# An attention output product made by token halves, one group to a unit

## The chip, the core and the metric

The program runs on one core of a Trainium2 chip. The core has five engines that work from queues of their own: TensorE (PE, matmuls; PEld is its weight load), VectorE (DVE), ScalarE (ACT), GpSimd (POOL) and SyncE (SP), which here only issues DMAs. Each queue runs in the order in which it was filled; engines wait for each other by semaphores. The metric is the device time of one execution in microseconds, the median of several runs. Before the change it is 1578.19 us (three runs, 1576.92 to 1581.11).

## What is computed

One layer of a diffusion transformer over 1024 latent tokens of width 1024 with 256 context tokens. What matters here is the token mixer: two attentions side by side, each of 8 query heads and 2 key heads of width 64, whose outputs are each multiplied by a weight, gated, added and multiplied by a third weight:

```python
o_a = _windowed_attention(q_a, k_a, v_a, k_a_c, v_a_c, sink)      # +-128 tokens and the context
o_b = _global_attention(q_b, k_b + context, v_b + context)        # all tokens and the context
g_a, g_b = jnp.split(jax.nn.sigmoid(gate_logits), 2, axis=-1)
return (g_a * (o_a @ w_branch_a) + g_b * (o_b @ w_branch_b)) @ w_out
```

Then come a residual with layer norm, a convolutional feed-forward block (1024 to 2 x 2816 to 1024) and a second residual with layer norm. All is float32; the kernel keeps that precision by splitting each operand into a high and a low part and using three matmuls for one (`mm3`, lines 89 to 91: high x high, high x low, low x high).

## The kernel before

The work runs in stages: the modulation and the input projections; the attention part; the merge of both attentions with `w_out`; the first layer norm; the feed-forward products; the last layer norm. The change is in the attention part.

The attention part is a list of 32 units (class `Unit`). A unit is one attention branch, one tile of 128 query tokens and one key head with its four query heads. Units 0 to 15 are the windowed branch (tile 0 key head 0, tile 0 key head 1, tile 1 key head 0, and so on), units 16 to 31 the global branch in the same order. For a unit the kernel makes scores on PE (`lat`, line 427, and for the global branch the context scores in `cxp`, line 463), scales them and finds maxima on DVE (line 458; 470 and 471 for the context), takes exponentials on ACT (line 425), and joins the two softmax parts (`norm`, line 478, with line 482 on DVE and line 486 on POOL). Then the probabilities of each 128 keys are transposed on PE (line 530) into a PSUM buffer of the tag `pt`, of which there are three, and split: ACT copies the high part (line 539), DVE subtracts it for the low part (line 540); two of the ten tiles of a global unit are instead copied by ACT (line 536) and split on POOL (lines 83 and 86). PE multiplies both with the values (lines 551 and 552). The result is put together and split on ACT, POOL and DVE (`out_step`, line 554), multiplied by the reciprocals of the row sums, which go through DRAM to be spread over partitions (`rows`, line 495, with DMAs on SP at lines 503 and 505), and stored in the tiles `O`. There are 12 buffers for `O`, while both branches together need 16 tiles, so that the tiles of the second half of the global branch reuse those of the first half of the windowed branch.

A loop over u (line 832) writes, for each u, the score steps of unit u, the preparation of the query of unit u + 2 (`qprep`, whose two halves are swapped by two DMAs on SP, lines 407 and 408), the value steps of the unit before, and filling steps, mixed by their fractions of the unit. DMAs that add blocks of the down-projection weights in DRAM (`wd_sums`) are issued at certain units.

The filling steps are the product of the windowed branch with its weight `w_branch_a`, from `branch_steps` (line 791). The weight comes in four blocks. `ld` loads one block (512 KB, tag `wraw`, one buffer) on SP and splits it on POOL into a high tile by a conversion (line 83) and a low tile by a subtraction (line 86), tag `whl` with two buffers, which is one block. `grp` makes one group: for one of eight output tiles of 128 channels and one half of 512 tokens it loads the stored gate (line 807, on SP), does four times three matmuls of 128x512 into a `pt` buffer and multiplies the result by the gate on DVE (line 814). With both halves in one list a block's steps are `ld` and four groups, twenty steps in all: sixteen groups and four loads. They are put in at u = 18 and spread over units 18 to 25, by steps (3, 3, 3, 3, 2, 2, 2, 2). At u = 31 the first block of the second branch's weight is loaded in the same buffers; its groups are made after the loop (line 867).

The order written here is not quite the order in which an engine runs. When the program is built, a planner goes through the written order with costs that it assumes for each instruction, and puts into each engine's queue what is ready, what was written earlier first. So a DMA or a split can stand far ahead of the unit in which it is written: the first weight block is loaded at 318.8 us and split at 349.7 us, well before unit 18. Only for the stages behind the attention part is PE's order the written one. On the chip, each queue then runs strictly in that order.

Of the kernel before, what the change touches and what calls it, by code (L numbers as in the profile page):

```python
# [30 lines left out]
VL = 1  # L31
NXT = 17
LAG = 3, 3
FILL_END = 26
XPOS = 2
SPAN = 0.8, 0.85
LN1_F = 3500.0, 5100.0, 100.0
# [29 lines left out]
def layer_kernel(  # L67
# [6 lines left out]
    nc = tc.nc  # L74
# [4 lines left out]
    def split(src, hi, lo, hi_eng, lo_eng):  # L79
        if hi_eng is nc.scalar:  # L80
            cast[:] = [nc.scalar.copy(hi, src).ins]  # L81
        elif hi_eng is nc.gpsimd:
            nc.gpsimd.tensor_scalar(out=hi, in0=src, scalar1=1.0, scalar2=0.0, op0=ALU.mult, op1=ALU.add)  # L83
        else:
            hi_eng.tensor_copy(hi, src)
        low[:] = [lo_eng.tensor_tensor(out=lo, in0=src, in1=hi.bitcast(F32), op=ALU.subtract).ins]  # L86

    def mm3(ps, a, b, start, stop, resumed=False):
        nc.tensor.matmul(ps, a[0], b[0], start=start, stop=False, skip_group_check=resumed)  # L89
        nc.tensor.matmul(ps, a[0], b[1], start=False, stop=False, skip_group_check=resumed)  # L90
        nc.tensor.matmul(ps, a[1], b[0], start=False, stop=stop, skip_group_check=resumed)  # L91
# [40 lines left out]
    def ht(name, shape=(P, T), dt=F32):  # L132
        hslot[name] = pool, tag = hfree.pop(0)
        return pool.tile(list(shape), dt, tag=tag, name=name, bufs=1)
# [623 lines left out]
    att = tc.alloc_tile_pool(name="att", bufs=1, side="right", reuse_waits="tile")  # L758
# [32 lines left out]
    def branch_steps(br, wsrc, halves, wpool, engs, f2s=range(4)):  # L791
        steps = []
        w = {}

        def ld(f2, key):
            r = wpool.tile([P, 8, P], F32, tag="wraw", name=f"rwb{br}_{key}", bufs=1)
            nc.sync.dma_start(r, wsrc[f2])
            h = wpool.tile([P, 8, P], R32, tag="whl", name=f"hwb{br}_{key}", bufs=2)
            l = wpool.tile([P, 8, P], R32, tag="whl", name=f"lwb{br}_{key}", bufs=2)
            split(r, h, l, *engs)  # L800
            w[f2] = h, l

        def grp(f, hf, mk):
            if (br, f) not in bT:
                bT[br, f] = ht(f"bT{br}_{f}")
            b = bT[br, f][:, hf * HALF:(hf + 1) * HALF]
            nc.sync.dma_start(b, sgd[br * KT + f][:, hf * HALF:(hf + 1) * HALF])
            wh, wl = w[f // 2]
            ps = mk(f"b{br}_{f}_{hf}")
            for j in range(4):  # L810
                k = (f % 2) * 4 + j
                a = O[br, hf, 0, j // 2][:, j % 2], O[br, hf, 1, j // 2][:, j % 2]
                mm3(ps, (wh[:, k], wl[:, k]), a, j == 0, j == 3)
            nc.vector.tensor_tensor(out=b, in0=ps, in1=b, op=ALU.mult)

        for f2 in f2s:
            steps.append(lambda f2=f2: ld(f2, f"{f2}_{halves[0]}"))
            for f in (2 * f2, 2 * f2 + 1):
                for hf in halves:
                    steps.append(lambda f=f, hf=hf: grp(f, hf, pt_tile))  # L820
        return steps

    def done(br, i, g):
        if g and i % 2:
            hput(f"Q{br}_{i - 1}")
        if g and i == NT - 1:
            hput(f"KL{br * 2}", f"KL{br * 2 + 1}")

    fill = []
    nu = len(units)  # L830
    vq = []
    for u in range(nu + 1):
        vs = []
        while vq and (vq[0] <= u - VL or vq[0] >= 16 or u >= 17):
            vs += units[vq.pop(0)].value_steps()
        ss = []
        if u < nu:
            ss = units[u].score_steps()
            if u + 2 < nu:
                ss.append(units[u + 2].qprep)  # L840
        if u == 31:
            first = branch_steps(1, w_b, (0, 1), att, (nc.gpsimd, nc.gpsimd), (0,))
            first[0]()
        if u == 18:
            fill += branch_steps(0, w_a, (0, 1), att, (nc.gpsimd, nc.gpsimd))
        nf = 0
        if u >= 18:
            nf = -(-len(fill) // (FILL_END - u)) if u < FILL_END else len(fill)
        fs = [fill.pop(0) for _ in range(nf)]
        if u < nu:  # L850
            ss = [units[u].context] + ss
        seq = []
        for lst, of, sp in ((ss, 0.0, SPAN[u >= 17]), (vs, VOFF, VSPAN), (fs, 0.0, 1.0)):
            for n, st_ in enumerate(lst):
                seq.append((of + sp * (n + 0.5) / len(lst), st_))
        for _, st_ in sorted(seq, key=lambda e: e[0]):
            st_()
        if u in DNS:
            wd_sums(*DNS[u])
        if u < nu:  # L860
            vq.append(u)
            done(units[u].br, units[u].i, units[u].g)
# [458 lines left out]
    for k in range(4):  # L1321
        steps = build(k)
        n = 2 if k < 2 else 0
# [278 lines left out]
    u, ot = [], []  # L1602
# [147 lines left out]
```

## Time and profile before

| what | value |
|---|---|
| median of the runs | 1578.19 us (1576.92 to 1581.11) |
| the profiled execution, its time | 1580.51 us |
| the profiled execution, its span | 1578.6 us |
| mean granted TensorE clock | 0.994 |
| start of the first windowed unit's output, `avs` | 364.6 us |
| global units 16 to 30, by the starts of their context reductions (line 470, DVE) up to that of unit 31 | 473.8 to 748.2 us |
| last unit's output, `avs` | 775.2 us |

The span runs from the first to the last instruction of the profiled execution. Views of the profile name an instruction by its line in the kernel, its engine, its operation and its tiles (`ptr<-ident,p` writes the tile `ptr` and reads the others; buffer numbers are left out). Where a line belongs to a helper, such as lines 81, 83 and 86 (the split) or 89 to 91 (the three matmuls), the tile tells which use it is: `hwb` and `lwb` are the high and low parts of a weight block of the branch products, `b` is the PSUM tile of a group, `bT` the gated result. A line of the waits says which instruction's engine sat idle until which other instruction ended, with the total, how often, and the longest. Busy time of PE comes from modelled ends, so that back-to-back matmuls overlap in it; the time from one start to the next is the better measure of what a matmul needs.

### The profile page before, as it was taken

How to read it: one execution, taken by the hardware profiler on the slowest of the kernel's cores; microseconds unless marked ns; L12 is line 12 of the kernel's file. 1: busy time of each engine (PE TensorE's matmuls, PEld its weight loads, DVE VectorE, ACT ScalarE, POOL GpSimd, SP SyncE). 2: the span in 40 equal slices, each digit the busy share in tenths (PEclk: the TensorE clock that was granted, in tenths of full speed). 3: DMA queues.
4: the chain of work that ended last, by engine and by line, in shares of the span. 5: the costliest groups of instructions: out<-in, count | busy, mean ns of one | idle time of the engine just before them, and what ended most of it. 6: DMA issues, size and time to landing. Idle time of an engine off the chain costs nothing.

```text
span 1578.6 us, 21930 instructions
## 1 busy us (share of the span) xinstructions
PE 1528.4 (97%) x7614; PEld 1264.6 (80%) x7614; DVE 1198.0 (76%) x1761; ACT 808.9 (51%) x1439; POOL 756.5 (48%) x737
## 2 busy tenths in 40 slices
PE   6999999999999999999999999999999999999997
PEld 5878788878886887777788898888888888888886
DVE  7797645628888777788675679888888888656797
ACT  5422222448888667688522466444444444435533
POOL 0573312426666566655432544666667765021053
PEclk9999999999999999999999999999999999999999
DMA  9685662322227555532344132333334446996723
GB/s 378 218 313 187 213 219 87 120 79 74 64 82 180 138 128 127 128 84 41 130 160 93 54 107 81 121 107 107 107 107 107 107 111 178 364 270 221 244 92 107
DMA packets 112015, 230.25 MB, mean 146 GB/s; under 512 B 13504, under 2 KB 27328, under 8 KB 111808
## 3 DMA queue, kind: packets, MB, share of 16 engines
q1 hardware_dynamic: 96464, 199.20, 37.9%
q0 software_dynamic: 10400, 20.19, 8.2%
q10 hardware_dynamic: 5040, 9.46, 1.6%
q8 instruction: 60, 0.98, 0.3%
q14 instruction: 51, 0.42, 0.1%
HBM read 177.61 MB, written 65.87 MB: 154 GB/s over the span
## 4 chain that ended last, share of the span: by engine, by line
PE 73%; DVE 12%; DMA 5%; ACT 4%; issue 3%; POOL 1%; SPq 0%; ACTq 0%; DVEq 0%; POOLq 0%
PE ptr L530 5%; PE b L91 3%; PE b L90 3%; PE b L89 3%; PE g L89 3%; PE g L91 3%; PE g L90 3%; PE s L413 2%; PE av L551 2%; PE c L90 2%; PE d L90 2%; PE a L90 2%; PE c L89 2%; PE d L89 2%; PE a L89 2%
## 5 line engine op out<-in xcount | busy, mean ns | idle before, releaser
L540 DVE TENSOR_TENSOR ptl<-ptr,pth 128x512 fp32r<-128x512 f32 x188 | 124.6, 684 | 27.8 <-ACT pth L539 25.6
L86 DVE TENSOR_TENSOR ld<-rd,hd 128x1024 fp32r<-128x1024 f32 x77 | 97.6, 1284 | 50.8 <-ACT hd L81 48.7
L530 PE MATMUL ptr<-ident,p 128*128 128x128 f32 x816 | 126.7, 278 | 9.2 <-DVE ptl L540 6.8
L539 ACT CAST pth<-ptr 128x512 fp32r<-128x512 f32 x188 | 106.5, 588 | 56.5 <-PE ptr L530 32.8
L425 ACT ACTIVATE p<-p,nm 128x1024 f32<-128x1024 f32 (+2 forms) x128 | 125.3, 981 | 11.1 <-DVE p L458 10.3
L530 PEld LDWEIGHTS ptr<-ident,p 128*128 128x128 f32 x816 | 93.6, 140 | 39.6 <-DVE ptl L540 13.9
L81 ACT CAST hd<-rd 128x1024 fp32r<-128x1024 f32 x77 | 79.4, 1050 | 88.5 <-PE p L91 60.4
L551 PE MATMUL av<-pth,VT 128*128 128x512 f32 x236 | 104.6, 443 | 1.0 <-ACT avs L557 0.5
L90 PE MATMUL p<-ld,hd 128*128 128x512 f32 x264 | 103.5, 392 | 0.3 <-DVE ld L86 0.3
L89 PE MATMUL p<-hd 128*128 128x512 f32 x264 | 103.8, 393 | 0.0
L91 PE MATMUL p<-hd,ld 128*128 128x512 f32 x264 | 103.5, 392 | 0.0
L89 PE MATMUL g<-hh,whg 128*128 128x512 f32 x256 | 99.9, 390 | 0.0
L91 PE MATMUL g<-hh,wlg 128*128 128x512 f32 x256 | 99.7, 389 | 0.0
L90 PE MATMUL g<-hl,whg 128*128 128x512 f32 x256 | 99.6, 389 | 0.0
L552 PE MATMUL av<-ptl,VT 128*128 128x512 f32 x236 | 97.7, 414 | 1.9 <-POOL ptl L86 1.8
L86 POOL TENSOR_TENSOR wlg<-wg,whg 128x512 fp32r<-128x512 f32 x32 | 44.2, 1388 | 112.7 <-ACT whg L81 109.2
L458 DVE TENSOR_SCALAR_CACHE_REDUCE p<-s,cvt,nmc 128x1024 f32<-128x1024 f32 x64 | 84.4, 1339 | 12.3 <-PE s L414 11.8
L413 PE MATMUL s<-KL,q 128*128 128x512 f32 (+2 forms) x192 | 76.0, 396 | 2.9 <-ACT p_x L425 2.0
L187 DVE CUSTOM_DVE_ANT_0 wml<-wml,sc,bmc 128x1024 f32<-128x1024 f32 x32 | 45.6, 1435 | 40.6 <-DMA wml<-in_wmodT_dram 39.7
L83 POOL TENSOR_SCALAR pth<-prw 128x512 fp32r<-128x512 f32 x48 | 31.0, 646 | 87.8 <-ACT prw L536 62.3
L414 PE MATMUL s<-KL,q 128*128 128x512 f32 (+2 forms) x192 | 71.7, 373 | 0.0
L81 ACT CAST wS<-s 128x512 fp32r<-128x512 f32 x76 | 45.3, 621 | 51.0 <-POOL s L1083 50.2
(402 smaller groups left out, 4945.7 us busy)
## 6 DMA issues: line engine op xcount, KB each, us to landing
wml<-in_wmodT_dram SPq DMA_DIRECT2D x48, 512.0 KB
ru<-in_w_up_dram SPq DMA_DIRECT2D x38, 512.0 KB
rd<-td SPq DMA_DIRECT2D x55, 256.0 KB
rd<-sd SPq DMA_DIRECT2D x44, 256.0 KB
rd<-in_w_dn_dram SPq DMA_DIRECT2D x33, 256.0 KB
wm<-in_wmodT_dram SPq DMA_DIRECT2D x16, 512.0 KB
wg<-in_w_g_dram SPq DMA_DIRECT2D x32, 256.0 KB
sgd<-sg ACTq DMA_DIRECT2D x32, 256.0 KB
```

What stands on the lines that cost most here:

```text
L81: cast[:] = [nc.scalar.copy(hi, src).ins]
L86: low[:] = [lo_eng.tensor_tensor(out=lo, in0=src, in1=hi.bitcast(F32), op=ALU.subtract).ins]
L89: nc.tensor.matmul(ps, a[0], b[0], start=start, stop=False, skip_group_check=resumed)
L90: nc.tensor.matmul(ps, a[0], b[1], start=False, stop=False, skip_group_check=resumed)
L91: nc.tensor.matmul(ps, a[1], b[0], start=False, stop=stop, skip_group_check=resumed)
L413: nc.tensor.matmul(o, self.q[0][:, hs], ks, start=True, stop=False)
L425: nc.scalar.activation(p, s, AF.Exp, bias=nm[:, h:h + 1], scale=scale, accum_out=sm[:, h:h + 1])
L530: nc.tensor.transpose(tr[:, h * P:(h + 1) * P], self.pslice(h, n), ident)
L539: nc.scalar.copy(hi, tr)
L540: nc.vector.tensor_tensor(out=lo, in0=tr, in1=hi.bitcast(F32), op=ALU.subtract)
L551: nc.tensor.matmul(self.av, v, hi, start=first, stop=False)
L552: nc.tensor.matmul(self.av, v, lo, start=False, stop=self.left == 0)
```

## The change

The product of the windowed branch is written as two lists, one for each half of the tokens, each with all four weight blocks: eight loads with their splits instead of four, and the same sixteen groups. A list has eight groups; the load of the next block is put behind each second group. The sixteen groups go into units 16 to 30, one each, and two into unit 27; the first half's groups are thus in units 16 to 23 and the second half's in units 24 to 30. The first block of the first half is loaded at unit 15, the first block of the second half with the last group of the first half, in unit 23.

```diff
@@ -31,7 +31,7 @@
 LAG = 3, 3
-FILL_END = 26
+FILL_G = {u: 1 + (u == 27) for u in range(16, 31)}
 XPOS = 2
@@ -841,12 +841,13 @@
         if u == 31:
             first = branch_steps(1, w_b, (0, 1), att, (nc.gpsimd, nc.gpsimd), (0,))
             first[0]()
-        if u == 18:
-            fill += branch_steps(0, w_a, (0, 1), att, (nc.gpsimd, nc.gpsimd))
-        nf = 0
-        if u >= 18:
-            nf = -(-len(fill) // (FILL_END - u)) if u < FILL_END else len(fill)
-        fs = [fill.pop(0) for _ in range(nf)]
+        fs = [st_ for _ in range(FILL_G.get(u, 0)) for st_ in fill.pop(0)]
+        if u == 15:
+            for hf in (0, 1):
+                st_ = branch_steps(0, w_a, (hf,), att, (nc.gpsimd, nc.gpsimd))
+                lds, grps = st_[0::3], [g for n, g in enumerate(st_) if n % 3]
+                fill += [[g] + lds[n // 2 + 1:n // 2 + 2] * (n % 2) for n, g in enumerate(grps)]
+                (fs if hf == 0 else fill[7]).append(lds[0])
         if u < nu:
             ss = [units[u].context] + ss
```

## The prediction, made before the changed kernel was run

> **What bounds the kernel now.** I read the page first, for the whole. Its first, engine and chain lines:
>
> ```profile
> span 1578.6 us, 21930 instructions
> PE 1528.4 (97%) x7614; PEld 1264.6 (80%) x7614; DVE 1198.0 (76%) x1761; ACT 808.9 (51%) x1439; POOL 756.5 (48%) x737
> PE 73%; DVE 12%; DMA 5%; ACT 4%; issue 3%; POOL 1%; SPq 0%; ACTq 0%; DVEq 0%; POOLq 0%
> ```
>
> TensorE is the bound over all, but the change touches only the global attention part, so I cut that part into stretches. Each global unit has one reduction over its context scores (line 470), and its starts in the timeline give the cuts: 473.8 (unit 16), 486.4, 503.0 (unit 18), 667.4 (unit 26), 748.2 (unit 31). The view of the stretches gives length, then busy time and number of instructions of PE, PEld, DVE, ACT and POOL, then clock, DMA share and GB/s; the second fence is the same view for the product tile `b` alone.
>
> ```profile
> 473.80:486.40 12.60, 10.60 (x63) 8.28 (x61) 11.06 (x18) 11.05 (x27) 8.66 (x11) 1.00 0.70 198
> 486.40:503.00 16.60, 15.53 (x87) 11.12 (x85) 13.95 (x26) 13.76 (x32) 12.67 (x20) 1.00 0.95 207
> 607.25:626.50 19.25, 18.48 (x107) 14.92 (x105) 14.14 (x23) 13.69 (x30) 12.60 (x15) 1.00 0.64 150
> 503.00:667.40 164.40, 161.36 (x905) 132.27 (x904) 121.48 (x214) 111.26 (x244) 95.63 (x131) 1.00 0.56 131
> 667.40:748.20 80.80, 74.83 (x442) 59.34 (x440) 70.99 (x117) 65.34 (x146) 47.70 (x67) 1.00 0.27 63
> ```
>
> ```profile
> 503.00:667.40 164.40, 47.64 (x192) 35.42 (x192) 11.02 (x16) 1.00 0.56 131
> 607.25:626.50 19.25, 2.97 (x12) 2.18 (x12) 0.69 (x1) 1.00 0.64 150
> 667.40:748.20 80.80, 0.00 (x0) 0.00 (x0) 0.00 (x0) 1.00 0.27 63
> ```
>
> All 192 matmuls of the product, 16 groups of 12, lie in the eight units 18 to 25. There PE is idle only 164.40 - 161.36 = 3.04 us, 0.38 a unit, and DVE is busy 74%. In the five units 26 to 30, which have no group, PE is idle 5.97 us, 1.19 a unit, and DVE is busy 88%: PE and DVE bound these together. Units 16 and 17 have no group either and leave 2.00 and 1.07 us. Clock is 1.00 throughout, so it plays no part.
>
> What PE waits for in units 26 to 30 (the view of the waits; the second line is the same wait over the twice as long stretch of units 18 to 25):
>
> ```profile
> PE ptr L530 <- DVE ptl L540: 3.9, 7, 1.1
> ...
> PE ptr L530 <- DVE ptl L540: 1.9, 3, 0.8
> ```
>
> So where no product runs, PE stands behind DVE, which subtracts the high part of a transposed tile (line 540) before the PSUM buffer is free. This is the time that the change could collect.
>
> **The change, part by part.**
>
> **1. The groups are spread.** No matmul, gate multiplication or gate load is added or removed: 16 groups, now one in each of units 16 to 30 and two in unit 27. What a group needs of PE when nothing else runs is seen at the end of the part, where groups of the second product follow each other; these are their DVE multiplications:
>
> ```profile
> 783.82 0.69 DVE L814 TENSOR_TENSOR bT<-b,bT 128x512 f32<-128x512 f32 x1 [0.77 <-PE b L91]
> 786.53 0.69 DVE L814 TENSOR_TENSOR bT<-b,bT 128x512 f32<-128x512 f32 x1 [0.90 <-PE b L91]
> ```
>
> 786.53 - 783.82 = 2.71 us. A unit without a group takes 80.80 / 5 = 16.16, one with two takes 164.40 / 8 = 20.55; so a group adds (20.55 - 16.16) / 2 = 2.19, and 0.52 of its 2.71 goes into time in which PE stood. Two in a unit recover 1.04, eight units 8.3 us in all. If a single group recovers 0.52, the spreading gains nothing; if the first recovers the whole 1.04, fifteen units recover 15.6 and the gain is 7.3. The one unit of before with a single group, 607.25 to 626.50, decides which is nearer: PE idle 19.25 - 18.48 = 0.77, just the middle of 1.19 and 0.38, which is the end without gain. Its edges are not sharp and units 16 and 17 have more to give, so I take a little above it, 0.6 a group-bearing unit: 15 x 0.6 - 8.3 = 0.7. **-0.7 us**, ends 0 and -7.3. With eight groups their gate multiplications on DVE (0.69 each) move into units 16, 17 and 26 to 30, where DVE is at 88%; each of these units also becomes some 2.2 us longer, which hides it. If it didn't, it would cost 8 x 0.69 = 5.5 us, which counts with the reshuffling below.
>
> **2. Blocks are loaded and split twice.** Before, 4 blocks of the first product; after, 8. Each is a 512 KB transfer on SP, a POOL conversion and a POOL subtraction. The view by tile, which also has the one block of the second product:
>
> ```profile
> L83 POOL TENSOR_SCALAR hwb<-rwb x5: 1042/1048/1058, 349.7 to 664.5; 128x1024 fp32r<-128x1024 f32 x5
> L86 POOL TENSOR_TENSOR lwb<-rwb,hwb x5: 2363/2396/2402, 350.9 to 668.4; 128x1024 fp32r<-128x1024 f32 x5
> L797 SPq DMA_DIRECT2D rwb<-in_w_a_dram x4: 333/352/537, 318.8 to 576.3; - x4
> ```
>
> Added on POOL: 4 x (1.05 + 2.40) = 13.8 us, over 274 us in which POOL has about 40% to spare (47.70 of 80.80 busy): hidden as POOL time. Added on SP: 4 x 0.35 us of issue. But the first block is split in the windowed part, at 350, before and after alike; so the global part goes from 4 subtractions (three blocks and that of the second product) to 8. What one does to others there is in the timeline:
>
> ```profile
> 541.55 2.40 POOL L86 TENSOR_TENSOR lwb<-rwb,hwb 128x1024 fp32r<-128x1024 f32 x1
> 572.68 2.40 POOL L86 TENSOR_TENSOR lwb<-rwb,hwb 128x1024 fp32r<-128x1024 f32 x1
> 614.16 2.40 POOL L86 TENSOR_TENSOR lwb<-rwb,hwb 128x1024 fp32r<-128x1024 f32 x1
> 668.41 2.39 POOL L86 TENSOR_TENSOR lwb<-rwb,hwb 128x1024 fp32r<-128x1024 f32 x1
> ```
>
> ```profile
> 542.02 1.95 DVE L482 TENSOR_TENSOR f<-nm,nmc 128x4 f32<-128x4 f32 x1
> 543.90 1.21 DVE L470 TENSOR_REDUCE nmc<-s_x 128x4 f32<-128x1024 f32 x1
> 668.61 2.21 DVE L471 TENSOR_TENSOR nmc<-nmc,cvt 128x4 f32<-128x4 f32 x1
> 670.74 1.27 DVE L540 TENSOR_TENSOR ptl<-ptr,pth 128x512 fp32r<-128x512 f32 x2
> ```
>
> ```profile
> L471 DVE TENSOR_TENSOR nmc<-nmc,cvt x16: 124/151/2206, 475.4 to 750.2; 128x4 f32<-128x4 f32 x16
> L482 DVE TENSOR_TENSOR f<-nm,nmc x16: 150/170/1948, 485.3 to 761.6; 128x4 f32<-128x4 f32 x16
> ```
>
> Two tiny DVE operations with both inputs in SBUF, median 0.15 and 0.17 us, took 2.21 and 1.95: they began inside a subtraction of POOL and ended with it (668.41 + 2.39 = 670.80; 541.55 + 2.40 = 543.95). Two of four subtractions met one, at 2.06 and 1.78 us of DVE. What reached PE:
>
> ```profile
> 544.74 0.50 PE L551 MATMUL av<-pth,VT 128*128 128x512 f32 x1 [0.31 <-ACT pth L539]
> 671.47 1.25 PE L530 MATMUL ptr<-ident,p 128*128 128x128 f32 x8 [1.12 <-DVE ptl L540]
> ```
>
> 0.31 in a unit with two groups, where PE had other work, and 1.12 in unit 26, which had none. After the change the units have one group. I price a hit at 1.12 and hits at two in four: 4 more subtractions x 0.5 x 1.12 = **+2.2 us**; ends 0 (none meets) and 4 x 2.06 = +8.2 (each meets one and all of it passes on). The Trainium skill, SBUF — State Buffer, section Who interferes with whom, has this as a rule: a VectorE instruction with two inputs in SBUF and a GpSimd instruction that reads SBUF exclude each other for the whole instruction; by it the added price would lie toward the upper end if the meetings were frequent, and the trace agrees on the two that it has.
>
> **3. Waits that come with the blocks.** There are two buffers for a split block (high and low), one for a raw one. A conversion therefore waits on POOL until PE is done with the last group of the block before, and the raw load behind it waits on SP for the subtraction (two lines of the waits, of POOL and of SP's queue, and one of the timeline):
>
> ```profile
> POOL hwb L83 <- PE b L90: 10.8, 2, 5.5
> ...
> SPq L797 <- POOL qs L83: 12.5, 1, 12.5
> ...
> 478.82 0.50 PE L552 MATMUL av<-ptl,VT 128*128 128x512 f32 x1 [1.38 <-POOL ptl L86]
> ```
>
> Four more of each. Queued behind the conversion on POOL are the two splits of tiles 2 and 6 of a unit (waited for by PE two steps later), the query split and the output of the unit; behind the load on SP are the query's swapped halves, used a unit later, and the row of reciprocals, used at the unit's end. In units 18 to 25 PE shows no wait on POOL at this, so I take **0**; the nearest row where POOL was late for PE is the last one above, 1.38, so the end is 4 x 1.38 = +5.5. The below-nothing end is 0: nothing is taken off these queues. The spacing after the change is kinder: a next group comes a unit (about 18 us) later, against 3.45 us for a split, save in unit 27, whose two groups stand on either side of a load, as in unit 21 before.
>
> **4. The end of the part.** The block of the second product was split at 664 to 671; it must now wait for the last group, in unit 30, and falls into unit 30 or 31, about 740 to 750. It is needed by the first group after the loop, at 774.96 before:
>
> ```profile
> 774.96 0.39 PE L89 MATMUL b<-O,hwb 128*128 128x512 f32 x1
> ...
> 779.63 0.50 PE L90 MATMUL b<-O,hwb 128*128 128x512 f32 x1 [0.21 <-POOL O L86]
> ```
>
> Some 25 us of room: **0**. If the split were put just ahead of the last unit's output on POOL, on which the last row waits, it would cost its 3.4 us; the other end is -1.1, the hit at 668.6 gone from unit 26. The output tiles of the first part that are reused by later units become free earlier (half 0 done in unit 23 instead of 25): nothing waited there, nothing is gained.
>
> **Sum:** -0.7 + 2.2 + 0 + 0 = **+1.5 us**. The profiled execution took 1580.51 us around its span of 1578.60; it would become 1582.0. It lies 2.3 above the median of the runs shown, 1578.19; from the median the sum gives 1579.7. I forecast 1579.5: no change by the bound of 0.3% (4.7 us, about what a measurement of this kernel can tell from none).
>
> **The rivals.**
> *Faster: the first group of a unit fills PE's gap.* DVE then catches up during the 2.71 us, recovery is 1.04 a unit, the gain 7.3, less 0 to 2.2 for the subtractions: -6, 1572. For it: DVE is the releaser in groupless units (3.9 us of waits) and nearly absent with two. Against: the single-group unit, which sat in the middle.
> *Slower: the exclusion of DVE by POOL.* If three of the four added subtractions, or more, meet a DVE operation and 1.5 us or more of each passes on, the price exceeds 4.7 + 0.7 and decides. At the full 8.2 less 0.7: +7.5, 1586. For it: units 26 to 30 are those with DVE at 88%, and the one hit there passed 1.12. Against: two of four had no meeting at all. By the page named above the lock is certain once they meet; how often they meet only the order decides.
> *Slower: POOL and SP late.* If each added block makes POOL late for PE once, +5.5, with the terms above +7: 1585. For it: POOL waited 5.5 us at a time. Against: no PE wait followed.
> *The groups don't move.* The order in an engine's queue is made by a planner. Before, those written in units 18 to 25 ran in just these units, so I give it nothing of its own.
>
> **How the numbers follow.** No change 0.47 (1574 to 1583), the faster rival 0.22, the lock 0.18, late POOL and SP or a planner's reshuffling 0.13. Faster 0.22, same 0.47, slower 0.31. The range reaches on one side to the faster rival with nothing lost to subtractions (1578.2 - 7.3 = 1571), on the other to the lock's 1586, and leaves out about a tenth on each side.
>
> **What would show it.** Step 1: groups evenly one to a unit, PE idle about 0.75 to 0.8 in each of units 18 to 30, units of some 18.3 us. Step 2: eight subtractions of 2.40 between 490 and 760, and about four DVE operations of 128x4 that take about 2 us. Step 3: more waits of the conversion on PE, none of PE on POOL at them. Step 4: the first group after the loop starts as PE ends the last unit. I am wrong if idle per unit falls to 0.4 (faster), or if PE waits for DVE after most subtractions, or if later stages change length: they should only shift.

## The result and the profile after

The changed kernel takes 1583.24 us, the kernel before in the same comparison 1578.26 (median of 14 runs each); the ratio is 1.0031, with a 95% interval of 1.0024 to 1.0038. So it became about 5.0 us slower, at the edge of the 4.7 us by which "no change" was defined. The forecast of 1579.5 was 3.7 us too low; the range, 1571 to 1586, holds the time. The profiled execution of after took 1583.69 us around a span of 1581.9. Its first, engine and chain lines:

```profile
span 1581.9 us, 21943 instructions
PE 1524.1 (96%) x7614; PEld 1263.3 (80%) x7614; DVE 1191.2 (75%) x1761; ACT 807.7 (51%) x1439; POOL 776.8 (49%) x745
PE 72%; DVE 12%; DMA 6%; issue 4%; POOL 3%; ACT 3%; SPq 0%; ACTq 0%; DVEq 0%; POOLq 0%
```

PE has the same 7614 matmuls, POOL has 8 instructions more (745 against 737, four conversions and four subtractions) and 20 us more busy time, and POOL's share of the chain that ended last went from 1% to 3%. The stretches, cut as before at the starts of the context reductions (line 470): unit 16, unit 17, unit 18, units 20 and 21, and units 16 to 30 together.

```profile
475.34:489.20 13.86, 12.37 (x70) 9.94 (x69) 10.81 (x19) 11.15 (x28) 7.45 (x10) 1.00 0.74 202
489.20:512.15 22.95, 17.55 (x99) 13.91 (x99) 13.99 (x27) 13.36 (x30) 17.75 (x22) 1.00 0.65 148
512.15:530.64 18.49, 17.67 (x103) 14.40 (x102) 14.68 (x25) 13.44 (x32) 10.42 (x15) 1.00 0.46 107
549.98:568.21 18.23, 17.61 (x102) 14.01 (x102) 14.77 (x26) 13.79 (x31) 10.43 (x16) 1.00 0.70 153
568.21:587.57 19.36, 17.52 (x103) 14.43 (x102) 15.49 (x26) 13.27 (x31) 13.93 (x17) 1.00 0.69 172
475.34:755.92 280.58, 260.71 (x1489) 211.09 (x1488) 219.38 (x371) 200.27 (x446) 179.07 (x234) 1.00 0.52 123
```

Units 16 to 30 took 274.4 us before (473.8 to 748.2, from the prediction's fence) and take 280.58 now: +6.2. The attention part as a whole, from the first `avs` of the windowed branch to the last gate multiplication of the second product's first block (364.6 to 786.5 before, 366.6 to 794.4 after), became 5.9 us longer. The span grew by only 3.3, because the stages ahead of it took 2.0 us more and those behind it 4.6 less in these two executions. The stages behind, which no edit here touches, took between 787.4 and 792.5 us in the profiles of all the kernels below, so a difference of a few microseconds is read from the attention part, not from the span. Where in the units the time went is worked out with the prices of before. There a group added 2.19 us to a unit, and two groups moved into units 16 and 17:

| stretch | before | after | difference | two groups at 2.19 moved | not explained by that |
|---|---|---|---|---|---|
| units 16, 17 | 29.20 | 36.81 | +7.6 | +4.4 | +3.2 |
| units 18 to 30 | 245.2 | 243.77 | -1.4 | -4.4 | +3.0 |

There are thus two losses of about the same size: one in unit 17, where PE stands 22.95 - 17.55 = 5.40 us (1.07 before), and one spread over the later units. In these a rhythm of two is seen: a unit without a split (18 and 20) takes 18.2 to 18.5 and PE stands 0.6 to 0.8; a unit with a split (21 in the fence; 19, 23 and 25 alike) takes 19.4 and PE stands 1.84. The waits of units 16 to 30 (who sat idle until what ended; total, times, longest):

```profile
POOL hwb L83 <- PE b L90: 26.6, 6, 5.8
DVE ot L562 <- POOL up L559: 16.7, 8, 2.6
...
PE ptr L530 <- DVE ptl L540: 11.4, 9, 2.3
```

The last two lines are a path from POOL to PE: DVE waits for a copy on POOL (6.2 us in units 16 to 30 before), and PE waits for DVE (5.8 before). The first line, POOL's conversion waiting for the last group of the block before, is the largest and looks like its start, but the timeline shows that it isn't. Here is unit 21, instruction by instruction (start, length, engine, line, tiles; in brackets the idle time ahead and what ended it):

```profile
574.72 1.06 POOL L83 TENSOR_SCALAR hwb<-rwb 128x1024 fp32r<-128x1024 f32 x1 [4.30 <-PE b L90]
575.86 2.39 POOL L86 TENSOR_TENSOR lwb<-rwb,hwb 128x1024 fp32r<-128x1024 f32 x1
578.93 0.62 POOL L559 TENSOR_SCALAR up<-avs 64x512 f32<-64x512 f32 x1
579.63 1.50 POOL L86 TENSOR_TENSOR ptl<-prw,pth 128x512 fp32r<-128x512 f32 x1
576.24 0.59 ACT L536 COPY prw<-ptr 128x512 f32<-128x512 f32 x1 [1.04 <-PE ptr L530]
576.72 0.59 ACT L557 COPY avs<-av 128x512 f32<-128x512 f32 x1
579.58 1.83 DVE L562 TENSOR_TENSOR ot<-avs,up 64x256 f32<-64x256 f32 x2 [2.43 <-POOL up L559]
581.45 1.89 DVE L540 TENSOR_TENSOR ptl<-ptr,pth 128x512 fp32r<-128x512 f32 x3
582.19 0.66 PE L530 MATMUL ptr<-ident,p 128*128 128x128 f32 x4 [1.84 <-DVE ptl L540]
585.45 1.48 POOL L86 TENSOR_TENSOR ptl<-prw,pth 128x512 fp32r<-128x512 f32 x1
586.71 0.90 POOL L86 TENSOR_TENSOR qs<-Q,qs 128x256 fp32r<-128x256 f32 x1
586.38 1.26 DVE L482 TENSOR_TENSOR f<-nm,nmc 128x4 f32<-128x4 f32 x1
```

POOL stands 4.30 us until 574.72, then converts and subtracts until 578.25. The stand itself costs nothing: what is queued behind needs ACT's copies `prw` and `avs`, which end at 576.83 and 577.31. What counts is that the split then occupies POOL for 1.4 us after `prw` is there (the same in units 19, 23 and 25). So the little copy `up` (line 559), queued behind, comes out only at 579.55. DVE has stood 2.43 us for it, with three low-part subtractions `ptl` (line 540) queued behind its `ot`. The first of these had its input from 578.9, the others from 580.1 and 580.8, and all three run from 581.45; so the PSUM buffers come free late, and PE stands 1.84. `ot` is itself long: two additions whose inputs both lie in SBUF, 0.42 us each by their median, take 1.83 here, because one of them begins within POOL's subtraction `ptl` (line 86) and ends 0.3 us after it. Such a long addition, 1.2 to 1.5 us, stands in 12 of the 15 units of after, in 8 of before, and also in 12 of the kernel of the first experiment below, which has no split in units 16 to 29. Later in the same unit the query's subtraction `qs` on POOL is late too, and DVE's `f`, 0.17 us by its median, is held to 1.26: it starts at 586.38, inside the subtraction `ptl`, and ends with `qs` at about 587.6.

### The profile page after: what moved, and what is told of

It is laid out like the page before. It is cut to its first block, busy times and chain, and to the rows that moved or that the text cites. A ratio compares the mean times of both kernels' runs of the same rounds, so it can differ in the third digit from the quotient of the medians.

```text
span 1581.9 us, 21943 instructions
## 1 busy us (share of the span) xinstructions
PE 1524.1 (96%) x7614; PEld 1263.3 (80%) x7614; DVE 1191.2 (75%) x1761; ACT 807.7 (51%) x1439; POOL 776.8 (49%) x745
## 4 chain that ended last, share of the span: by engine, by line
PE 72%; DVE 12%; DMA 6%; issue 4%; POOL 3%; ACT 3%; SPq 0%; ACTq 0%; DVEq 0%; POOLq 0%
PE ptr L530 4%; PE b L90 3%; PE b L89 3%; PE b L91 3%; PE p L89 2%; PE p L91 2%; PE p L90 2%; PE d L89 2%; PE c L89 2%; PE a L89 2%; PE c L90 2%; PE d L90 2%; PE a L90 2%; PE c L91 2%; PE d L91 2%
## 5 line engine op out<-in xcount | busy, mean ns | idle before, releaser
L81 ACT CAST wA<-ru 128x512 fp32r<-128x512 f32 x57 | 35.5, 623 | 60.7 <-PE d L91 32.4
```

## The experiments

Two things had to be told apart: whether the loss comes with the four added splits or with the new places of the groups; and, for the splits, whether it is POOL's lateness in its queue, the exclusion between DVE and POOL, or simply that a split costs its time wherever it is put. All ratios are to the kernel before, which was run again beside each set of experiments (medians of 1578.04 to 1579.31), so two experiments are best compared by their ratios; "the units' sum" is units 16 to 30 in the profile, 274.4 before and 280.6 after; "the attention part" is its difference to before in the profile, +5.9 for after.

**Groups spread, no later blocks.**

```diff
+    bw = {}
...
-            wh, wl = w[f // 2]
+            if br == 0 and not bw:
+                bw.update(w)
+            wh, wl = bw[0] if br == 0 else w[f // 2]
...
-                fill += [[g] + lds[n // 2 + 1:n // 2 + 2] * (n % 2) for n, g in enumerate(grps)]
-                (fs if hf == 0 else fill[7]).append(lds[0])
+                fill += [[g] for g in grps]
+                if hf == 0:
+                    fs.append(lds[0])
```

> The changed kernel with only the first weight block loaded and split (before the global part); all sixteen groups multiply with this one block, so the product is not the reference's. Groups, their places, the gates and the first block of the second product stay. Theory A (each split on GpSimd in a one-group unit makes the unit's output parts late, VectorE stands behind them, and TensorE behind VectorE, about 1.1 us for a split): the units with a split, 19.4 us against 18.2 without, all become 18.2; five such units and unit 27, and part of unit 17's excess, so 6 to 9 us less than the changed kernel, 1574 to 1577. Theory B (the spreading itself costs, one group to a unit recovers less of TensorE's idle time): the long units stay long, 1583 within 1.5 us.

Measured: 1577.73 us, ratio 0.9995 (0.9985 to 1.0005); units' sum 275.2, attention part +0.7. The stretch of units 17 and 19 of this kernel:

```profile
487.14:508.16 21.02, 17.56 (x99) 13.96 (x99) 13.49 (x27) 13.45 (x30) 14.30 (x20) 1.00 0.63 135
526.64:545.14 18.50, 17.69 (x103) 14.40 (x102) 14.65 (x25) 13.43 (x32) 10.37 (x15) 1.00 0.59 135
```

The 5 us are gone: with the groups in their new places and the later splits away the kernel is as fast as before, a little above theory A's 1574 to 1577. Units 18 to 26 are now all alike, 18.44 to 18.51 us, with PE idle 18.50 - 17.69 = 0.81. A split in after thus costs what a pair of units differs by: 19.36 + 18.23 - 2 x 18.47 = 0.65 us. Unit 17 is still long, 21.02 with 3.46 us of PE idle, so something there doesn't come from a split.

**Four splits fewer: the second half keeps the first half's last block.**

```diff
+    bw = {}
...
-            wh, wl = w[f // 2]
+            if br == 0 and hf == 0:
+                bw[0] = w[f // 2]
+            wh, wl = w[f // 2] if br or hf == 0 else bw[0]
...
-                fill += [[g] + lds[n // 2 + 1:n // 2 + 2] * (n % 2) for n, g in enumerate(grps)]
-                (fs if hf == 0 else fill[7]).append(lds[0])
+                fill += [[g] + (lds[n // 2 + 1:n // 2 + 2] * (n % 2) if hf == 0 else []) for n, g in enumerate(grps)]
+                if hf == 0:
+                    fs.append(lds[0])
```

> The changed kernel without the second load and split of the weight blocks: the second half's groups multiply with the last block of the first half, so the product is not the reference's. Four splits less, as many as before the change. Theory A: the four units in which they lay (23, 25, 27, 28) give back 1.1 us each, units 19 and 21 stay at 19.4: 4 to 5 us less than the changed kernel, 1578 to 1579.5, about the kernel before. Theory B: 1583 within 1.5 us.

Measured: 1583.89 us, ratio 1.0029 (1.0018 to 1.0039); units' sum 278.7, attention part +4.1. In the profile the attention part is 1.9 us shorter than in after, 0.47 for each of the four splits, and units 23 and 25 fall from 19.4 to 18.4 and 18.5. The median doesn't show it: theory A's 1578 to 1579.5 is missed, and 1583.89 is what theory B gave. The interval of the ratio is 0.21% wide, 3.3 us, and the profiled execution, 1580.09, is the fastest of the eleven; so this run confirms the size in the profile and leaves open whether the time follows.

**The splits ordered behind the output of the unit on POOL.** The aim was to let `up` and the output go ahead of the conversion and its wait. `olast` holds the last operation of a unit's output split.

```diff
+                olast[:] = low
...
+    olast = []
...
-            split(r, h, l, *engs)
+            if br == 0 and key != "0_0":
+                with tc.issue_after(olast[0]):
+                    split(r, h, l, *engs)
+            else:
+                split(r, h, l, *engs)
```

> The changed kernel with all its splits, but each split of the first product's blocks (save the very first) ordered on GpSimd behind the last operation of the unit's output. Theory A: the waits of TensorE of 1.84 us in units 19, 21, 23 and 25 and of 2.25 us in unit 17 go, units of 18.2 to 18.5 us throughout, 5 to 8 us less than the changed kernel, 1575 to 1578. Theory C (it is GpSimd's occupation as such, or its exclusion of VectorE by the long subtraction, wherever the split stands): 1581 to 1584, with VectorE operations of about 2 us elsewhere.

Measured: 1602.56 us, ratio 1.0153 (1.0137 to 1.0170); units' sum 297.7, attention part +23.1. A clear miss: the change of order that was to take the loss away cost 19 us more. The timeline of one split, POOL and DVE and the wait that follows on PE:

```profile
585.52 2.02 DVE L482 TENSOR_TENSOR f<-nm,nmc 128x4 f32<-128x4 f32 x1
587.61 2.61 POOL L86 TENSOR_TENSOR lwb<-rwb,hwb 128x1024 fp32r<-128x1024 f32 x1
589.97 2.03 POOL L486 TENSOR_SCALAR p_x<-p_x,f 128x256 f32<-128x256 f32 x4
591.78 0.90 POOL L86 TENSOR_TENSOR qs<-Q,qs 128x256 fp32r<-128x256 f32 x1
589.19 3.51 DVE L487 TENSOR_TENSOR smc<-smc,f 128x4 f32<-128x4 f32 x1
593.84 1.09 PE L530 MATMUL ptr<-ident,p 128*128 128x128 f32 x4 [3.15 <-DVE ptl L540]
```

The DVE operation `smc` (line 487, also two SBUF inputs of 128x4, 0.16 us by its median here) begins at 589.19 inside the subtraction and ends only at 592.70, after four pieces of the scaling `p_x` and with the query's subtraction `qs`, which follow each other on POOL. In this order POOL's long operations stand where `f` and `smc` run. Another row of the same kernel, of the tile `f` (min, median and maximum in ns):

```profile
L482 DVE TENSOR_TENSOR f<-nm,nmc x16: 149/368/4025, 489.3 to 786.8; 128x4 f32<-128x4 f32 x16
```

Three `f` took 3.99 to 4.03 us; in all, six of the eight subtractions met an `f` or an `smc`. So the exclusion that step 2 feared is real, and a meeting can hold DVE for much longer than the 2.06 us that was the upper end there.

Not all of the 19 us is that, though. The lines of units 20 and 24 of this kernel, neither of which leaves PE idle more than 0.13 us:

```profile
550.59:568.04 17.45, 17.32 (x100) 13.74 (x100) 15.25 (x26) 12.78 (x28) 10.79 (x16) 1.00 0.66 166
631.34:650.40 19.06, 18.93 (x104) 15.68 (x105) 14.75 (x27) 13.49 (x30) 10.98 (x16) 0.91 0.59 137
```

In unit 24 the granted clock is 0.91, and so it is in units 22 (0.92), 26 (0.91) and 27 (0.87), each time behind one of PE's long waits, of 2.0 to 3.15 us; waits of 2.99 and 1.96 had no such sequel. (Unit 24 also has four matmuls more than unit 20, at most 0.9 us by the 0.23 from one start to the next.) In after no wait of PE in these units is above 2.25 us, and the clock stays at 1.00. Of the 17.1 us by which units 16 to 30 exceed those of after (297.66 against 280.58), 9.0 are more idle time of PE and 8.1 more busy time for the same matmuls, which goes with the lower clock. All five executions have a mean clock of 0.987 to 0.992, those of every other kernel here 0.992 or more.

**Halves with eight splits, in the old places.** Two groups to each of units 18 to 25.

```diff
-FILL_G = {u: 1 + (u == 27) for u in range(16, 31)}
+FILL_G = {u: 2 for u in range(18, 26)}
```

> The second part of the change alone: token halves with eight loads and splits, but the groups in units 18 to 25, two to each, as in the kernel before. Theory A: units with two groups give TensorE more other work, so each added split costs 0.3 to 1.1 us: 1579.5 to 1583. Theory B: no cost from splits, 1577 to 1579.5, the kernel before.

Measured: 1582.15 us, ratio 1.0022 (1.0013 to 1.0031); units' sum 276.8, attention part +1.9. The doubling alone costs 0.22% or 3.5 us, and 1.9 us in the profile's attention part: 0.5 there for each of the four added splits. Here the exclusion is seen: five of the eight subtractions met an `f`, which took 1.94 to 2.03 us each time, and a sixth met an `nmc` of 1.48. How much of the 1.9 us is due to it isn't shown; PE's idle time in units 16 to 30 grew by only 0.8 us (12.07 to 12.91), and POOL's conversions waited 0.6 us in all. One of the pairs (DVE and POOL in the timeline):

```profile
521.49 2.37 POOL L86 TENSOR_TENSOR lwb<-rwb,hwb 128x1024 fp32r<-128x1024 f32 x1
521.85 2.03 DVE L482 TENSOR_TENSOR f<-nm,nmc 128x4 f32<-128x4 f32 x1
```

The Trainium skill, SBUF — State Buffer, section Who interferes with whom, has such a pair exclude each other; the trace agrees: `f` ends at 523.88 and the subtraction at 523.86.

**Groups in units 18 to 30 only.** All eight splits, none of the groups in units 16 and 17, two in units 21, 24 and 27.

```diff
-FILL_G = {u: 1 + (u == 27) for u in range(16, 31)}
+FILL_G = {u: 1 + (u in (21, 24, 27)) for u in range(18, 31)}
```

> The changed kernel with the groups in units 18 to 30 only (two in units 21, 24 and 27), units 16 and 17 without one as before the change. Theory A2 (a group in units 16 and 17 makes the planner put GpSimd's second accumulating DMA ahead of the context probabilities, where it stands for the first DMA; this and the split in unit 17 are the largest single loss): units 16 and 17 return to 12.6 and 16.6 us, 7.6 less, the moved groups cost 2 x 2.2 elsewhere: 3 us less than the changed kernel, 1580. Theory B (one group to a unit is what costs, wherever it is): no more than 1 us less, 1582 to 1584.

Measured: 1578.04 us, ratio 0.9999 (0.9990 to 1.0007); units' sum 274.0, attention part -0.3. Units 16 and 17:

```profile
473.46:486.09 12.63, 10.57 (x63) 8.28 (x61) 11.11 (x18) 11.06 (x27) 8.68 (x11) 1.00 0.67 198
486.09:502.55 16.46, 15.35 (x87) 11.15 (x85) 13.96 (x26) 13.80 (x33) 12.71 (x20) 1.00 0.96 208
```

They are as before, 12.63 and 16.46. With eight splits the kernel is level with the kernel before, so the places of two groups out of sixteen are worth as much as all the added splits. But the losses aren't a fixed price each: units 18 to 30 take 244.9 us here with sixteen groups and eight splits, and 240.4 with fourteen groups and one split in the kernel with one block, a difference that two groups at 2.19 make up. So the 0.65 of a split is the price in the steady pairs of after, and not a price in any order. POOL's conversions wait 32.0 us for PE here, more than in after, and it costs nothing. Why unit 17 costs so much is in POOL's timeline there. After:

```profile
492.15 1.17 POOL L600 DMA_DIRECT2D sd<-in_w_dn_dram  x1 [2.99 <-DMA sd<-in_w_dn_dram]
492.87 2.32 POOL L486 TENSOR_SCALAR p_x<-p_x,f 128x256 f32<-128x256 f32 x4
494.69 1.75 POOL L86 TENSOR_TENSOR ptl<-prw,pth 128x512 fp32r<-128x512 f32 x1
496.53 0.62 POOL L559 TENSOR_SCALAR up<-avs 64x512 f32<-64x512 f32 x1
501.31 2.39 POOL L86 TENSOR_TENSOR lwb<-rwb,hwb 128x1024 fp32r<-128x1024 f32 x1
```

Before, at the same place:

```profile
486.85 1.84 POOL L486 TENSOR_SCALAR p_x<-p_x,f 128x256 f32<-128x256 f32 x4 [0.39 <-ACT f L483]
488.78 0.61 POOL L559 TENSOR_SCALAR up<-avs 64x512 f32<-64x512 f32 x1
490.64 1.17 POOL L600 DMA_DIRECT2D sd<-in_w_dn_dram  x1 [1.25 <-DMA sd<-in_w_dn_dram]
```

Line 600 is the second, accumulating DMA of a weight sum (`wd_sums`, issued at unit 16). It waits for the first to land. Before, it stood behind the scaling `p_x` and the copy `up`; with a group written into unit 16 the planner put it ahead of them, and POOL stood 2.99 us with both of them behind it.

**The first weight sums a unit earlier.** After, with its groups where they are.

```diff
-        if u in DNS:
-            wd_sums(*DNS[u])
+        if u == 15:
+            wd_sums(*DNS[16])
+        elif u in DNS and u > 16:
+            wd_sums(*DNS[u])
```

> The changed kernel with the first weight sums in DRAM, written at unit 16, written at unit 15 instead, so that GpSimd's second accumulating DMA stands ahead of unit 17's work and its transfers are earlier. Theory A2 (this DMA issue, waiting 3.0 us at the head of GpSimd's queue in unit 17, makes 2 of the 6 us by which units 16 and 17 are too long): unit 17 at 20 to 21 us in place of 22.95, 1580 to 1582. Theory A3 (the groups and the split fill GpSimd and TensorE in unit 17 whatever the DMA does): 22.5 us or more, 1583.

Measured: 1580.47 us, ratio 1.0006 (0.9996 to 1.0015); units' sum 277.0, attention part +2.6. Unit 17 of this kernel:

```profile
488.00:507.52 19.52, 17.32 (x99) 13.77 (x99) 15.02 (x27) 13.50 (x30) 17.02 (x21) 1.00 0.53 123
```

It falls from 22.95 to 19.52, by 3.4 us, which is the attention part's whole gain (5.9 - 2.6 = 3.3); the ratio falls from 1.0031 to 1.0006. The place of that DMA issue is thus shown to be worth about half of the loss in the profile. The issue still waits, 3.87 us, but now in unit 16, ahead of the query's split, which itself had to wait for PE. The transfers moved with it, so that the run doesn't tell POOL's stand from the traffic in unit 17.

**The splits on ScalarE and VectorE.**

```diff
-                st_ = branch_steps(0, w_a, (hf,), att, (nc.gpsimd, nc.gpsimd))
+                st_ = branch_steps(0, w_a, (hf,), att, (nc.scalar, nc.vector))
```

> The changed kernel with the splits of the first product's blocks made on ScalarE (high part) and VectorE (low part) instead of GpSimd. Theory A (GpSimd being late for the unit's output is what costs): TensorE's waits of 1.84 us in units 19, 21, 23, 25 go; VectorE and ScalarE get about 1.25 and 1.05 us a block, which units of 18.4 us hide in part: 1578 to 1581. Theory C (a split costs its time on whatever engine it is put): 1583 or more.

Measured: 1581.70 us, ratio 1.0027 (1.0017 to 1.0037); units' sum 278.1, attention part +3.6. Of the 2.4 us that the profile gained over after, 1.5 are in unit 17 (21.44 for 22.95), where in after POOL has a split behind its wait. In the four steady pairs, units 19 to 26, the units with a split take 19.4 to 19.5 and the others 17.7 to 18.0: 37.4 a pair on average (37.20 to 37.55) against 36.94 without a split, so 0.4 a split, where POOL's cost 0.65. So about a third of a steady split's price goes with its place on POOL; the rest comes on these two engines as well. The time lies between the two theories, and the ratios, 1.0027 and 1.0031, don't tell this kernel from after.

**The copy `up` on ScalarE.** If DVE's stand at `ot` is the step by which a late POOL reaches PE, it should go when `up` doesn't come from POOL. First everywhere, with the same edit on the kernel before as control.

```diff
-                nc.gpsimd.tensor_scalar(out=up, in0=avs[HD:P], scalar1=1.0, scalar2=0.0, op0=ALU.mult, op1=ALU.add)
+                nc.scalar.copy(up, avs[HD:P])
```

> The changed kernel with the copy of the output's upper half (up<-avs) on ScalarE instead of GpSimd, so that VectorE's output addition no longer waits behind a split in GpSimd's queue. Theory A: VectorE's waits for it (16.7 us in units 16 to 30) and TensorE's 1.84 us waits in units 19, 21, 23, 25 go; ScalarE has 5 us a unit to spare; 3 to 5 us less than the changed kernel, 1578 to 1580. Theory C (the split's length itself, through the tiles split on GpSimd or its exclusion of VectorE): units 19 to 25 keep 19.4, 1582 to 1584.

> The kernel before with the same copy on ScalarE, as the control for the run above. If the copy's place matters by itself and not for the splits, this gains as much; theory A: less, 0 to 2 us, 1576 to 1578.5, since before the change only three splits stood in units of two groups each.

Measured: on after 1585.09, ratio 1.0045 (1.0031 to 1.0058); on before 1586.62, ratio 1.0055 (1.0039 to 1.0072). In both, the windowed units became some 8 to 9 us longer, which the edit wasn't for, while the units 16 to 30 fell to 271.7 and 273.9. So the times don't answer the question. In unit 17 they leave a hint: units 16 and 17 together fell from 36.8 to 34.0 us on after, unit 17 alone to 18.52, although the DMA issue still waits there 2.42 us, while on before the same edit made them 2.7 longer. Then in the global units alone (`if self.br`), again with a control:

> The changed kernel with the copy of the output's upper half (up<-avs) on ScalarE in the global units only, so that the windowed part keeps the changed kernel's time. With the copy on ScalarE throughout, units 16 to 30 took 271.7 us against 280.6, and the windowed part 8.3 us more. Theory A: the 8.9 us stay and the loss goes: 1574 to 1575.5, below the kernel before. If the global part's gain was a result of its late start: 1578 or more.

> The kernel before with the copy on ScalarE in the global units only, the control. Theory A: with two groups to a unit and only three splits little is to be had, 0 to 1 us: 1577 to 1578.5. If the copy's place alone is what gains, as low as the runs above.

Measured: on after 1578.92, ratio 0.9998 (0.9988 to 1.0008), units' sum 274.7, attention part +0.2. On before 1578.38, ratio 0.9991 (0.9981 to 1.0000), units' sum 274.7, attention part +0.3. The edit is worth 0.33% on after (1.0031 to 0.9998, 5.2 us) and at most 0.19% on before. Two units of the first, 19 and 25, which have a split each:

```profile
527.23:544.53 17.30, 16.87 (x98) 13.69 (x97) 13.99 (x25) 13.30 (x31) 12.39 (x16) 1.00 0.68 166
636.37:653.72 17.35, 16.90 (x98) 13.71 (x97) 14.07 (x26) 13.30 (x31) 12.41 (x15) 1.00 0.75 192
```

A unit with a split, 19.4 in after, is now 17.3 in units 19, 23 and 25, with PE idle 0.4. Units 23 and 24 together, and 25 and 26, take 35.3 us against 37.6 in after and 36.9 without splits, so they gain more than their split cost. Units 21 and 22 stay long, 19.04 and 19.72; in 21 an addition of `ot` meets the block's subtraction (1.43 us), and in 22 an `smc` is held to 2.19. It isn't a gain of the copy's place in every unit: 18 and 29, with one group and no split, take 18.40 and 18.43, where after took 18.49 in both, although `ot` in unit 18 fell from 1.91 to 0.85 us. Freeing `ot` of POOL's `ptl` is thus worth 0.1 there. The control frees `ot` as well (long additions in 1 unit for 8) and gains little. The new order that the planner makes with this edit is part of what is measured, and isn't separated. Unit 17 stays at 22.9, but the edit doesn't reach it: the two copies that run in it, at 493.21 and 501.04, belong to the last windowed units and are still POOL's, and DVE waits 4.7 us for them.

**Both remedies.** Groups in units 18 to 30 and `up` on ScalarE in the global units:

```diff
-FILL_G = {u: 1 + (u == 27) for u in range(16, 31)}
+FILL_G = {u: 1 + (u in (21, 24, 27)) for u in range(18, 31)}
...
-                nc.gpsimd.tensor_scalar(out=up, in0=avs[HD:P], scalar1=1.0, scalar2=0.0, op0=ALU.mult, op1=ALU.add)
+                if self.br:
+                    nc.scalar.copy(up, avs[HD:P])
+                else:
+                    nc.gpsimd.tensor_scalar(out=up, in0=avs[HD:P], scalar1=1.0, scalar2=0.0, op0=ALU.mult, op1=ALU.add)
```

> As the run above, with the groups in units 18 to 30 only. If units 16 and 17 cost for GpSimd's lateness alone, which the copy on ScalarE takes away, starting at 18 gains nothing more: 1574 to 1576. If a group in them costs for another reason (the DMA traffic there), 2 us or more less than the run above.

Measured: 1576.05 us, ratio 0.9973 (0.9961 to 0.9984); attention part -2.6. Its units 16 to 30:

```profile
476.14:748.00 271.86, 261.02 (x1490) 211.28 (x1488) 209.01 (x372) 209.26 (x462) 170.52 (x222) 1.00 0.54 127
```

271.86 against 274.4 before. This kernel is faster than both, by 0.27% against before and, by the two ratios, 0.58% or some 9 us against after, still with eight splits. It is 2.9 us below the run with `up` on ScalarE in the global units alone; by its expectation that points to another reason than POOL's lateness in units 16 and 17, but since that run left unit 17's copies on POOL, this isn't decided. Unit 17 takes 18.48 us here against 16.46 with the copy on POOL, and in the control 18.83 against 16.60; so the edit isn't free at its first units.

One combination wasn't tried: each block loaded and split once, with its groups spread up to unit 30. The tiles `O` of the first half would have to be kept longer (16 buffers for 12), or two split blocks at a time; whether SBUF has room for either isn't shown.

## Why the prediction was right and wrong

**The forecast and its sum.** The sum was +1.5 us; the runs gave +5.0. The range held it because it reached to the rivals on the slower side, and of these the one with POOL and SP late (1585, at a chance of 0.13 with the planner's reshuffling) describes the course best: POOL became late, and the planner moved something. But the rival had POOL late for PE, with PE waiting on POOL, which didn't happen. That the time lies in the range is therefore in part luck.

**Step 1, the groups spread, -0.7.** The groups went where they were to go, and a unit with one group came out as foreseen: 18.5 us against 18.3, PE idle 0.81 against 0.75 to 0.8. The recovery of a single group was set at 0.6; the kernel with one block gives 16.16 + 2.71 - 18.47 = 0.40. So the reading of the one half-way unit was sound, and the addition made to it was not. In the profile the spread with one block gives +0.8 us (units' sum 275.2 against 274.4, with three splits fewer than before), in the median -0.6 (1577.73 against 1578.34): nothing, as the lower end of step 1 had it, though the wait at line 600 in unit 17, 3.1 us, is still in it. The faster rival is refuted by the same unit: 18.47 isn't 16.16 + 2.71 - 1.04 = 17.8. With the copy moved off POOL, units 19, 23 and 25 do reach 17.3 and PE's idle time in the pairs falls to 0.5; so the gap can be filled in another order.

**Step 2, the exclusion, +2.2.** Eight subtractions ran, at 501 to 752 us, and 2.39 to 2.40 us each, as said. But four DVE operations of about 2 us were forecast, and none of the eight met one of 128x4. What did happen is one step removed: in the four split units 19, 21, 23 and 25 the transposed tile's and the query's subtractions on POOL came late and held `f` to 1.26 to 1.32 us. And the step counted only the blocks' subtractions and the operations of 128x4; the additions `ot` met POOL's `ptl` in 12 units for 8 before, at about 1.0 us of DVE each, which came with the groups' new places and cost next to nothing where it could be seen alone (0.1 us in unit 18). The row of `f` before is in the prediction (150/170/1948); this is the one after:

```profile
L482 DVE TENSOR_TENSOR f<-nm,nmc x16: 151/210/1325, 489.1 to 769.4; 128x4 f32<-128x4 f32 x16
```

The longest is down from 1.95 to 1.33, the median up from 0.17 to 0.21. The frequency of meetings, two in four, was the weak number: the order decides it, and in other orders it was none (after), six in eight (halves in units 18 to 25, five of them with `f`), or six in eight with up to 4.0 us each (splits behind the output). The condition of the rival built on this step was also set too low: three meetings at 1.5 us make 4.5, which is less than the 5.4 that it had to exceed.

**Step 3, waits that come with the blocks, 0.** This step failed. The first part was right: POOL's conversion waited more, six times for 26.6 us (10.8 in two before), and this wait indeed cost nothing. But the split behind it did: it keeps POOL 1.4 us past the moment at which the next work is ready. The conclusion "PE shows no wait on POOL at this, so 0" was wrong, since the lateness doesn't reach PE by a wait on POOL. It goes by DVE: `up` on POOL, `ot` on DVE, and `ptl` behind `ot` in DVE's queue, and PE's wait is put down to DVE, 11.4 us in nine waits. The step did list the output of the unit among what is queued behind the conversion, and didn't ask who stands in line behind the engine that waits for it. That the second group of a unit was the cover in before, as work for PE while DVE was late, is likely and not shown: with two groups to a unit an added split still cost 0.5 in the profile. The price was 0.65 a steady split. The end given, +5.5, holds the 5.4 us by which the units' sum of after exceeds that without the splits (280.6 - 275.2), by luck: it was worked out from a wait of PE on POOL.

Step 3 also looked only at the queues' added work, not at what the planner would do with work that was already there. The wait at line 600 in unit 17 was in the profile before, 1.25 us at a place where it did no harm, and it was not priced; the kernel with the sums a unit earlier has a unit 17 shorter by 3.4 us. Step 1 had even counted on units 16 and 17 having more to give than the others; unit 17 took.

**Step 4, the end of the part, 0.** Right. The second product's block was subtracted at 752.2 us, from the start of unit 31 to the last `avs` it took 27.1 us (26.9 before), and from there to the last group 11.40 (11.38 before).

**What is settled and what isn't.** Shown by moving it or taking it away: the place of the DMA issue of line 600 in unit 17 (3.4 us in the profile, 0.25% in the ratio), and the splits together (5.4 us of the units' sum; the two overlap in unit 17). Shown with a control: that most of the splits' loss goes when `up` leaves POOL (5.9 us of units 18 to 30 on after, 1.9 on before), with the planner's new order as a part that isn't separated. Open: why a split costs nothing measurable in units 18 to 30 when two more of them have two groups; how much of the 0.4 us that a split costs on ScalarE and VectorE is which engine's; and whether four splits fewer in the second half give any time, where profile and median didn't agree.

## What to carry to other kernels

When work is added to an engine off the critical path, it isn't enough that nobody on that path waits for it: follow who waits for what it will delay, and what stands behind that waiter in its own in-order queue, down to the engine that is the bound. Before work is moved into a place that looks idle, look at the waits that are there already: two groups in units 16 and 17 brought a loss that leaving these units alone gave back whole. Where a planner orders the queues, a DMA issue that waits on a compute engine's queue can be moved ahead of ready work by an edit elsewhere, so such issues belong in the sum.

## What was not expected of the hardware

A DVE operation with two SBUF inputs that begins inside a POOL instruction doesn't always get through when that instruction ends. In the kernel with the splits behind the output, `smc` of 0.16 us stayed for 3.51 us, over the subtraction, the scaling and the query's subtraction, and three `f` of 0.17 took 3.99 to 4.03, over the block's subtraction and that of a transposed tile, against 2.9 us for the longest single subtraction there. Before the change the longest had been 2.21, the rest of one subtraction, from which the upper end of step 2 (2.06 a hit) had been taken. A small case stood in the profile before all the same: an `f` of 1.36 us in unit 26 begins at 682.43 inside a tile's subtraction, which ends at 683.06, and ends with the query's at about 683.8.

The granted clock, 1.00 in units 16 to 30 of before and after, fell for some microseconds behind three of PE's waits of 3.0 to 3.15 us and one of 2.0 in that same kernel, so that its units 24 and 26 took 19.1 us with PE hardly idle. That the waits brought it about is likely and not shown by an experiment; if so, a wait of PE costs more there than its own length.
